# Attention steps on TensorE placed by shares of their stage's filling products

## The chip, the cores and the metric

The kernel runs on one core of one Trainium2 chip. The metric is the device time of one execution in microseconds (us); lower is better. The names of the engines are those of the profile: PE is TensorE, DVE is VectorE, ACT is ScalarE, POOL is GpSimd, SP issues the DMAs.

## The reference

One decoder block on 512 tokens of width 1024 in float32. A combined projection feeds two attention branches, multi-head latent attention (MLA, 8 heads) and differential attention (4 heads with two softmax maps each); their outputs are gated, merged and projected, and a SwiGLU layer of 2816 hidden channels follows.

```python
def apply_rope(x, positions, rot_dim):
...
def causal_attention(q, k, v):
...
def reference(...):
    xn = rmsnorm(x, norm_mix_g[l])
    proj = jnp.einsum('bsd,de->bse', xn, w_in[l])
    q_lat, kv_lat, k_rope, dq, dk, dv, gate_pre = jnp.split(proj, split_idx, axis=-1)
    q = jnp.einsum('bsr,re->bse', rmsnorm(q_lat, mla_q_norm_g[l]), mla_w_uq[l])
    kv = jnp.einsum('bsr,re->bse', rmsnorm(kv_lat, mla_kv_norm_g[l]), mla_w_ukv[l])
    ...
    o_mla = causal_attention(q_mla, k_mla, v_mla).reshape(B, S, MLA_WIDTH)
    ...
    o1 = causal_attention(dq[..., 0, :], dk[..., 0, :], dv)
    o2 = causal_attention(dq[..., 1, :], dk[..., 1, :], dv)
    ...
    o_diff = rmsnorm(o1 - lam * o2, diff_subln_g[l]) * (1.0 - lambda_init)
    gates = jax.nn.sigmoid(gate_pre + b_gate[l])
    merged = (g_mla * jnp.einsum('bse,ed->bsd', o_mla, w_branch_mla[l])
              + g_diff * jnp.einsum('bse,ed->bsd', o_diff, w_branch_diff[l]))
    x = x + jnp.einsum('bsd,de->bse', merged, w_out[l])
    hn = rmsnorm(x, norm_ffn_g[l])
    hid = jax.nn.silu(jnp.einsum('bsd,df->bsf', hn, w_ffn_gate[l])) * jnp.einsum('bsd,df->bsf', hn, w_ffn_up[l])
    x = x + jnp.einsum('bsf,fd->bsd', hid, w_ffn_down[l])
    return rmsnorm(x, norm_final_g)
```

## The kernel before

**Arithmetic.** Every large product is made of three matmuls in a rounded 32-bit format: the weights and the activations are each split into a high and a low part, and `mm3` (L299) issues high by high, high by low and low by high into one accumulation. A weight tile (512 KB or less) is loaded by SP into `raw`, its high part rounded by one engine (L264 or L266) and its low part formed by another (L269) into `w`. `w_eng` says which: DVE and POOL in the MLA stages, ACT and DVE in the differential stages.

**Stages.** After the start (input, latents, rotary tables) come four MLA stages, one for each pair of heads, and four differential stages, one for each head (loops at L807 and L819). Each stage traces its *filling products* first (`fill`, tables `FILL_MLA` and `FILL_DIFF`, L52 to L59): projections for later stages, 24 matmuls for each block of 128 columns of the input projection. Then it traces its *head steps* in an `urgent` block: `mla_head` twice, or `diff_norm` of the head before and `diff_head`. A head consists of four scores steps (`scores`, L624, one for each block of 128 queries, each followed by a reduction for the row maximum on DVE (L637), an exponential on ACT (L156) and a reciprocal (L640)), three groups of transposes (`transposed`, L651), each split on ACT and DVE, and the product with the values (`values` or the loop at L779). Behind the last stage the branch projections, the output projection and the SwiGLU layer follow, which are nearly all products.

**Order.** The program is written in tiles, and a scheduler puts each engine's instructions into one fixed order before the program runs. It takes what it holds ready by its own timeline, and among that what has the smaller priority number. `urgent` gives the head steps small numbers (from 1000), the rest counts from 1000000. So a head step goes ahead of any filling product as soon as the scheduler holds it ready. `tc.issue_after(x)` adds an edge: what is traced inside it stands behind `x` on `x`'s engine. The engines execute their orders strictly, and wait by semaphores.

**Buffers.** PSUM has three buffers for products (`ps_mm`), two for scores (`ps_sc`), two for transposes (`ps_tr`) and one for values (`ps_pv`). A step that needs a buffer waits until its last reader is done: a `ps_mm` of a differential query or key until the rotation (`rotate`, L562) has read it, which is a shuffle (L564) and a product (L565) on DVE; a `ps_sc` until the reduction at L637 has read it.

Of the kernel before, what the change touches and what calls it, by code (L numbers as in the profile page):

```python
# [93 lines left out]
def build(ctx, nc, tc, a, out):  # L94
# [176 lines left out]
    def weights(src, n0, n1, pick=None):  # L271
# [25 lines left out]
        return [w[:, i, :n].rearrange("p (a b) -> p a b", a=n0) for i in range(2)]  # L297

    def mm3(o, lhs, rhs, start, stop):  # L299
        (lh, ll), (rh, rl) = lhs, rhs  # L300
        nc.tensor.matmul(out=o, lhsT=lh, rhs=rh, start=start, stop=False)  # L301
        nc.tensor.matmul(out=o, lhsT=lh, rhs=rl, start=False, stop=False)  # L302
        return nc.tensor.matmul(out=o, lhsT=ll, rhs=rh, start=False, stop=stop)  # L303

# [318 lines left out]

    def scores(maps, i):  # L624


        n = (i + 1) * P
        pss = [PS("sc") for _ in maps]
        last = len(maps[0][0]) - 1
        for j in range(last + 1):  # L630
            for ps, (products, _) in zip(pss, maps):
                q, k = products[j]
                nc.tensor.matmul(out=ps[:, :n], lhsT=q[:, i * P:n], rhs=k[:, 0:n], start=j == 0, stop=j == last)  # L633
        rs = []
        for ps, (_, m) in zip(pss, maps):
            neg_max, s, r = sm(), sm(), sm()
            nc.vector.tensor_tensor_reduce(out=m, in0=ps[:, :n], in1=mask[:, S - n:], scale=-1.0, scalar=3.4e38,  # L637
                                           op0=ALU.add, op1=ALU.min, accum_out=neg_max)
            last_exp[0] = log_exp(out=m, in_=m, func=AF.Exp, bias=neg_max, scale=-1.0, accum_out=s)
            nc.vector.reciprocal(out=r, in_=s)  # L640
            rs.append(r)
        return rs
# [7 lines left out]

    def transposed(blocks):  # L651

        pt = T("PT", [P, 2, 1280], F32R)
        for js in ((0,), (1,), (2, 3)):
            ps = PS("tr")
            c = 0
            for j in js:
                for i in range(j, NB):
                    nc.tensor.transpose(out=ps[:, c:c + P], in_=blocks[i][:, j * P:(j + 1) * P], identity=ident)  # L659
                    c += P  # L660
            o0 = OFF[js[0]]
            split(ps[:, :c], pt[:, 0, o0:o0 + c], pt[:, 1, o0:o0 + c])
        return pt

    def values(pt, v):

        ps = PS("pv")
        for n_, (vs, s) in enumerate(((0, 0), (0, 1), (1, 0))):
            for j in range(NB):
                nc.tensor.matmul(out=ps[:, j * P:S], lhsT=v(j, vs), rhs=pt[:, s, OFF[j]:OFF[j] + S - j * P],  # L670
                                 start=n_ == 0 and j == 0, stop=n_ == 2 and j == NB - 1)
        return ps
# [6 lines left out]

    def diff_head(h, products):  # L680
        blocks = []
        for i, p1 in enumerate(prob_tiles()):
            p2 = T("P", [P, S], F32)[:, :(i + 1) * P]
            r1, r2 = scores(list(zip(products, (p1, p2))), i)
            nc.vector.tensor_mul(out=r2, in0=r2, in1=neg_lam)
            nc.scalar.activation(out=p2, in_=p2, func=AF.Copy, scale=r2)
            nc.vector.scalar_tensor_tensor(out=p1, in0=p1, scalar=r1, in1=p2, op0=ALU.mult, op1=ALU.add)
            blocks.append(p1)
        pt = transposed(blocks)
        ps = values(pt, lambda j, s: dv[(h // 2) * 2 + j // 2][:, s, (j % 2) * 256 + (h % 2) * P:  # L690
                                                              (j % 2) * 256 + (h % 2) * P + P])
        o32, sq = tmp(), tmp()
# [7 lines left out]

    def diff_norm(o32, sqs):

        ps = PS("tr")
        for s in range(2):
            nc.tensor.matmul(out=ps, lhsT=ones_r, rhs=sqs[s], start=s == 0, stop=s == 1)
        y, u = tmp(), tmp()
# [58 lines left out]

    def mla_head(qk, v, pair, o, h):
        q, k = qk[h]
        blocks = []
        for i, p in enumerate(prob_tiles()):
            r, = scores([([(q[0:96, a_, :], k[0:96, b_, :]) for a_, b_ in ((0, 0), (0, 1), (1, 0))], p)], i)  # L770
            if i in P_POOL:
# [3 lines left out]
            blocks.append(p)  # L775
        pt = transposed(blocks)
        c = 2 * (pair % 2) + h
        ps = PS("pv")
        for s in range(2):  # L779
            for j in range(NB):  # L780
                nc.tensor.matmul(out=ps[:, j * P:S], lhsT=v[j // 2][:, j % 2, c, :, :].rearrange("p s d -> p (s d)"),
                                 rhs=pt[:, s, OFF[j]:OFF[j] + S - j * P], start=s == 0 and j == 0,
                                 stop=s == 1 and j == NB - 1)
        u = tmp()[:64]
# [22 lines left out]
    for p in range(4):  # L807
        o = L_()
        o_mla.append(o)
        w_eng[:] = W_ENG  # L810
        fill(FILL_MLA[p])
        with urgent():
            for h in range(2):
                mla_head(mqk[p], mv[p // 2], p, o, h)
# [3 lines left out]
    w_eng[:] = W_ENG_DIFF  # L818
    for h in range(4):  # L819
        fill(FILL_DIFF[h])  # L820
        with urgent():
            if h > 0:
                o_diff.append(diff_norm(*parts[h - 1]))
            parts.append(diff_head(h, qk[h]))
    with urgent():
        o_diff.append(diff_norm(*parts[3]))

# [173 lines left out]
```

## Time and profile before

| | us |
|---|---|
| median of 3 runs | 751.91 (751.88 to 752.78) |
| the profiled execution, its own time | 753.9 |
| the profiled execution, span from first to last instruction | 752.1 |
| PE busy | 737.0 |
| DVE busy | 414.7 |
| ACT busy | 326.8 |
| MLA and differential stages, about | 75 to 310 |
| output projection and SwiGLU layer, about | 310 to 752 |

A row of the profile names a line of the kernel, an engine, an operation, the tile written and the tiles read. Busy time of PE counts each matmul until its result has drained, which overlaps with the start of the next; the pace of PE is read from the starts of successive matmuls. A 128x512 matmul has 0.39 us as its duration, and the next starts 0.23 us after it.

### The profile page before, as it was taken

To read this page: it belongs to the slowest core of one execution; us is meant where nothing else is said; L and a number is where in the kernel's file an instruction comes from. 1 tells how busy PE (TensorE), PEld (TensorE's weight loads), DVE (VectorE), ACT (ScalarE), POOL (GpSimd) and SP (SyncE) were. 2 spreads that over 40 slices of the span, in tenths; PEclk is the share of its full clock that TensorE was granted. 3 is DMA by queue.
4 is the path that set the end of the run, shared out by engine and by line. 5 is a ranking of instruction groups with operands and counts; after the bars stand their busy time and mean duration, and the time that the engine had idled before them with its cause. 6 is when DMAs were issued, how large, how long until landed. Compare 5 with 4: busy or idle time off the path is not lost.

```text
span 752.1 us, 9652 instructions
## 1 busy us (share of the span) xinstructions
PE 737.0 (98%) x3639; PEld 623.0 (83%) x3639; DVE 414.7 (55%) x800; ACT 326.8 (43%) x609; POOL 104.3 (14%) x94
## 2 busy tenths in 40 slices
PE   7999999999999999999999999999999999999996
PEld 5988889888888888788898888888888888888885
DVE  6968688898998745595453323333333332122424
ACT  6564558587667535644233323232322223122314
POOL 3505252631341001000000000000000000000302
PEclk9999999999999999999999999999999999999999
DMA  8404333552433322248023333333323232322203
GB/s 300 124 1 117 106 87 96 135 126 69 110 87 87 107 85 85 84 140 278 2 85 108 89 97 99 98 99 87 109 85 111 85 112 85 109 88 92 106 0 113
DMA packets 99820, 76.74 MB, mean 102 GB/s; under 512 B 6303, under 2 KB 86973, under 8 KB 99773
## 3 DMA queue, kind: packets, MB, share of 16 engines
q1 hardware_dynamic: 99773, 76.12, 34.3%
q8 instruction: 29, 0.48, 0.3%
q14 instruction: 18, 0.15, 0.1%
HBM read 69.81 MB, written 2.10 MB: 96 GB/s over the span
## 4 chain that ended last, share of the span: by engine, by line
PE 81%; DVE 9%; ACT 5%; POOL 2%; issue 2%; DMA 1%; SPq 0%; DVEq 0%; ACTq 0%
PE ps_mm L301 22%; PE ps_mm L303 22%; PE ps_mm L302 22%; PE ps_sc L633 2%; PE ps_sc L301 1%; PE ps_sc L302 1%; PE ps_tr L301 1%; PE ps_tr L302 1%; PE ps_tr L303 1%; PE ps_sc L303 1%; POOL t L567 1%; PE ps_tr L659 1%; ACT L L495 1%; DVE w L269 1%; DVE X L355 1%
## 5 line engine op out<-in xcount | busy, mean ns | idle before, releaser
L302 PE MATMUL ps_mm<-X,w 128*128 128x512 f32 (+1 forms) x568 | 217.0, 382 | 0.0
L301 PE MATMUL ps_mm<-X,w 128*128 128x512 f32 (+1 forms) x568 | 216.9, 382 | 0.1
L303 PE MATMUL ps_mm<-X,w 128*128 128x512 f32 (+1 forms) x568 | 216.6, 382 | 0.0
L269 DVE TENSOR_TENSOR w<-raw,w 128x1024 fp32r<-128x1024 f32 x92 | 116.3, 1266 | 165.4 <-ACT w L264 165.2
L264 ACT ACTIVATE w<-raw 128x1024 fp32r<-128x1024 f32 (+1 forms) x98 | 101.1, 1036 | 181.2 <-issue 78.9
L303 PEld LDWEIGHTS ps_mm<-X,w 128*128 128x128 f32 x568 | 106.9, 188 | 19.9 <-POOL w L269 0.3
L301 PEld LDWEIGHTS ps_mm<-X,w 128*128 128x128 f32 x568 | 106.7, 188 | 19.9 <-DVE t L565 0.2
L302 PEld LDWEIGHTS ps_mm<-X,w 128*128 128x128 f32 x568 | 106.8, 188 | 19.7 <-DVE X L255 0.2
L936 POOL TENSOR_TENSOR L<-L,P 128x512 f32<-128x512 f32 (+1 forms) x9 | 11.6, 1299 | 439.0 <-ACT t L935 439.0
L909 ACT ACTIVATE t<-ps_mm 128x512 f32<-128x512 f32 x22 | 13.2, 598 | 80.9 <-PE ps_mm L303 80.9
L910 DVE TENSOR_TENSOR t<-t,ps_mm 128x512 f32<-128x512 f32 x22 | 15.1, 688 | 59.7 <-PE ps_mm L303 59.7
L156 ACT ACTIVATE P<-P,sm 128x128 f32<-128x128 f32 (+3 forms) x64 | 35.8, 560 | 27.4 <-DVE sm L637 27.0
L269 POOL TENSOR_TENSOR w<-raw,w 128x1024 fp32r<-128x1024 f32 (+3 forms) x22 | 37.3, 1701 | 57.5 <-PE ps_tr L472 25.8
L633 PE MATMUL ps_sc<-L,L 96*128 96x128 f32 (+7 forms) x160 | 36.5, 327 | 1.5 <-DVE sm L637 1.5
L302 PE MATMUL ps_mm<-w,L 128*128 128x512 f32 (+1 forms) x100 | 37.2, 372 | 0.0
L301 PE MATMUL ps_mm<-w,L 128*128 128x512 f32 (+1 forms) x100 | 37.2, 374 | 0.0
L303 PE MATMUL ps_mm<-w,L 128*128 128x512 f32 (+1 forms) x100 | 37.1, 373 | 0.0
L301 PE MATMUL ps_mm<-L,w 128*128 128x512 f32 x90 | 35.2, 393 | 0.5 <-ACT w L264 0.5
L302 PE MATMUL ps_mm<-L,w 128*128 128x512 f32 x90 | 35.5, 394 | 0.0
L303 PE MATMUL ps_mm<-L,w 128*128 128x512 f32 x90 | 35.2, 393 | 0.0
L251 ACT ACTIVATE L<-t 64x512 fp32r<-64x512 f32 (+2 forms) x47 | 29.1, 623 | 13.6 <-POOL t L567 6.2
L255 DVE TENSOR_TENSOR L<-t,L 128x512 fp32r<-128x512 f32 (+2 forms) x37 | 29.6, 801 | 4.8 <-ACT L L251 4.5
(265 smaller groups left out, 1231.9 us busy)
## 6 DMA issues: line engine op xcount, KB each, us to landing
raw<-w_in SPq DMA_DIRECT2D x28, 512.0 KB, 4.0
raw<-w_ffn_gate SPq DMA_DIRECT2D x22, 512.0 KB, 3.9
raw<-w_ffn_up SPq DMA_DIRECT2D x22, 512.0 KB, 3.9
raw<-w_ffn_down SPq DMA_DIRECT2D x22, 512.0 KB, 3.6
L<-L SPq DMA_DIRECT2D x32, 128.0 KB, 2.9
raw<-w_out SPq DMA_DIRECT2D x8, 512.0 KB, 3.7
L<-x SPq DMA_DIRECT2D x8, 256.0 KB, 6.1
raw<-w_branch_mla SPq DMA_DIRECT2D x4, 512.0 KB, 3.4
```

The source lines that it names most:

```text
L156: return nc.scalar.activation(**kw)
L251: nc.scalar.activation(out=hi, in_=src, func=AF.Copy, scale=scale)
L255: nc.vector.tensor_sub(out=lo, in0=src, in1=r32(hi))
L264: nc.scalar.activation(out=o, in_=i, func=AF.Copy)
L269: (nc.vector if w_eng[1] == 'dve' else nc.gpsimd).tensor_sub(out=o, in0=i, in1=r32(hi))
L301: nc.tensor.matmul(out=o, lhsT=lh, rhs=rh, start=start, stop=False)
L302: nc.tensor.matmul(out=o, lhsT=lh, rhs=rl, start=False, stop=False)
L303: return nc.tensor.matmul(out=o, lhsT=ll, rhs=rh, start=False, stop=stop)
L633: nc.tensor.matmul(out=ps[:, :n], lhsT=q[:, i * P:n], rhs=k[:, 0:n], start=j == 0, stop=j == last)
L909: last_silu = nc.scalar.activation(out=g, in_=gate_ps, func=AF.Silu)
L910: nc.vector.tensor_mul(out=g, in0=g, in1=ps)
L936: nc.gpsimd.tensor_mul(out=xs, in0=xs, in1=g)
```

## The change

Each stage now keeps a list of its filling products (`units`, the last matmul of each `mm3`; emptied at the start of a stage). Each head step on PE is traced inside `paced(at)`, which is an `issue_after` edge to the product that stands at the share `at` of that list. For an MLA pair the shares are 0 to 0.54 for the first head and 0.28 to 0.97 for the second, so that the second head's steps stand between those of the first. For differential heads the four scores steps have 0, 0.14, 0.28 and 0.42, the transposes 0.7, 0.7 and 0.8, the values 0.95 (all times 0.6 for the last head), and the norm of the head before 0.2, 0.2 and 0.12; the norm of the last head has 0.75. A share of 0 adds no edge. Nothing that is computed changes.

```diff
@@ -296,11 +296,19 @@
             n = n0 * nk
         return [w[:, i, :n].rearrange("p (a b) -> p a b", a=n0) for i in range(2)]
 
+    units = []
+
     def mm3(o, lhs, rhs, start, stop):
         (lh, ll), (rh, rl) = lhs, rhs
         nc.tensor.matmul(out=o, lhsT=lh, rhs=rh, start=start, stop=False)
         nc.tensor.matmul(out=o, lhsT=lh, rhs=rl, start=False, stop=False)
-        return nc.tensor.matmul(out=o, lhsT=ll, rhs=rh, start=False, stop=stop)
+        units.append(nc.tensor.matmul(out=o, lhsT=ll, rhs=rh, start=False, stop=stop))
+        return units[-1]
+
+    def paced(at):
+
+        n = int(at * len(units))
+        return tc.issue_after(units[n - 1].ins) if n > 0 else nullcontext()
 
     def norm_transpose(xt, g, dst, t, junk):
 
@@ -621,7 +629,7 @@
         return kpe
 
 
-    def scores(maps, i):
+    def scores(maps, i, at):
 
 
         n = (i + 1) * P
@@ -630,7 +638,8 @@
         for j in range(last + 1):
             for ps, (products, _) in zip(pss, maps):
                 q, k = products[j]
-                nc.tensor.matmul(out=ps[:, :n], lhsT=q[:, i * P:n], rhs=k[:, 0:n], start=j == 0, stop=j == last)
+                with paced(at):
+                    nc.tensor.matmul(out=ps[:, :n], lhsT=q[:, i * P:n], rhs=k[:, 0:n], start=j == 0, stop=j == last)
         rs = []
         for ps, (_, m) in zip(pss, maps):
             neg_max, s, r = sm(), sm(), sm()
@@ -648,27 +657,29 @@
         for i in (2, 3):
             yield T("P", [P, S], F32)[:, :(i + 1) * P]
 
-    def transposed(blocks):
+    def transposed(blocks, at):
 
         pt = T("PT", [P, 2, 1280], F32R)
-        for js in ((0,), (1,), (2, 3)):
+        for at_, js in zip(at, ((0,), (1,), (2, 3))):
             ps = PS("tr")
             c = 0
             for j in js:
                 for i in range(j, NB):
-                    nc.tensor.transpose(out=ps[:, c:c + P], in_=blocks[i][:, j * P:(j + 1) * P], identity=ident)
+                    with paced(at_):
+                        nc.tensor.transpose(out=ps[:, c:c + P], in_=blocks[i][:, j * P:(j + 1) * P], identity=ident)
                     c += P
             o0 = OFF[js[0]]
             split(ps[:, :c], pt[:, 0, o0:o0 + c], pt[:, 1, o0:o0 + c])
         return pt
 
-    def values(pt, v):
+    def values(pt, v, at):
 
         ps = PS("pv")
         for n_, (vs, s) in enumerate(((0, 0), (0, 1), (1, 0))):
             for j in range(NB):
-                nc.tensor.matmul(out=ps[:, j * P:S], lhsT=v(j, vs), rhs=pt[:, s, OFF[j]:OFF[j] + S - j * P],
-                                 start=n_ == 0 and j == 0, stop=n_ == 2 and j == NB - 1)
+                with paced(at):
+                    nc.tensor.matmul(out=ps[:, j * P:S], lhsT=v(j, vs), rhs=pt[:, s, OFF[j]:OFF[j] + S - j * P],
+                                     start=n_ == 0 and j == 0, stop=n_ == 2 and j == NB - 1)
         return ps
 
 
@@ -677,18 +688,18 @@
     eps = sb.tile([P, 1], F32, name="eps")
     nc.gpsimd.memset(eps, EPS)
 
-    def diff_head(h, products):
+    def diff_head(h, products, span):
         blocks = []
         for i, p1 in enumerate(prob_tiles()):
             p2 = T("P", [P, S], F32)[:, :(i + 1) * P]
-            r1, r2 = scores(list(zip(products, (p1, p2))), i)
+            r1, r2 = scores(list(zip(products, (p1, p2))), i, span * (0, 0.14, 0.28, 0.42)[i])
             nc.vector.tensor_mul(out=r2, in0=r2, in1=neg_lam)
             nc.scalar.activation(out=p2, in_=p2, func=AF.Copy, scale=r2)
             nc.vector.scalar_tensor_tensor(out=p1, in0=p1, scalar=r1, in1=p2, op0=ALU.mult, op1=ALU.add)
             blocks.append(p1)
-        pt = transposed(blocks)
+        pt = transposed(blocks, (span * 0.7, span * 0.7, span * 0.8))
         ps = values(pt, lambda j, s: dv[(h // 2) * 2 + j // 2][:, s, (j % 2) * 256 + (h % 2) * P:
-                                                              (j % 2) * 256 + (h % 2) * P + P])
+                                                              (j % 2) * 256 + (h % 2) * P + P], span * 0.95)
         o32, sq = tmp(), tmp()
         nc.scalar.activation(out=o32, in_=ps, func=AF.Copy)
         nc.scalar.activation(out=sq, in_=ps, func=AF.Square)
@@ -698,11 +709,12 @@
         nc.gpsimd.tensor_sub(out=sqs[1], in0=sq, in1=r32(sqs[0]))
         return o32, sqs
 
-    def diff_norm(o32, sqs):
+    def diff_norm(o32, sqs, at):
 
         ps = PS("tr")
         for s in range(2):
-            nc.tensor.matmul(out=ps, lhsT=ones_r, rhs=sqs[s], start=s == 0, stop=s == 1)
+            with paced(at):
+                nc.tensor.matmul(out=ps, lhsT=ones_r, rhs=sqs[s], start=s == 0, stop=s == 1)
         y, u = tmp(), tmp()
         log_exp(out=y, in_=ps, func=AF.Ln, scale=1.0 / P, bias=eps)
         last_exp[0] = log_exp(out=y, in_=y, func=AF.Exp, scale=-0.5)
@@ -764,23 +776,27 @@
         return v
 
     def mla_head(qk, v, pair, o, h):
+
+        at = ((0, 0.07, 0.14, 0.21, 0.36, 0.36, 0.43, 0.54), (0.28, 0.46, 0.58, 0.65, 0.8, 0.8, 0.86, 0.97))[h]
         q, k = qk[h]
         blocks = []
         for i, p in enumerate(prob_tiles()):
-            r, = scores([([(q[0:96, a_, :], k[0:96, b_, :]) for a_, b_ in ((0, 0), (0, 1), (1, 0))], p)], i)
+            r, = scores([([(q[0:96, a_, :], k[0:96, b_, :]) for a_, b_ in ((0, 0), (0, 1), (1, 0))], p)], i,
+                         at[i])
             if i in P_POOL:
                 nc.gpsimd.tensor_scalar(out=p, in0=p, scalar1=r, scalar2=0.0, op0=ALU.mult, op1=ALU.add)
             else:
                 nc.scalar.activation(out=p, in_=p, func=AF.Copy, scale=r)
             blocks.append(p)
-        pt = transposed(blocks)
+        pt = transposed(blocks, at[4:7])
         c = 2 * (pair % 2) + h
         ps = PS("pv")
         for s in range(2):
             for j in range(NB):
-                nc.tensor.matmul(out=ps[:, j * P:S], lhsT=v[j // 2][:, j % 2, c, :, :].rearrange("p s d -> p (s d)"),
-                                 rhs=pt[:, s, OFF[j]:OFF[j] + S - j * P], start=s == 0 and j == 0,
-                                 stop=s == 1 and j == NB - 1)
+                with paced(at[7]):
+                    nc.tensor.matmul(out=ps[:, j * P:S], lhsT=v[j // 2][:, j % 2, c, :, :].rearrange("p s d -> p (s d)"),
+                                     rhs=pt[:, s, OFF[j]:OFF[j] + S - j * P], start=s == 0 and j == 0,
+                                     stop=s == 1 and j == NB - 1)
         u = tmp()[:64]
         nc.scalar.activation(out=u, in_=ps[64:P, :], func=AF.Copy)
         nc.vector.tensor_add(out=u, in0=ps[0:64, :], in1=u)
@@ -808,6 +824,7 @@
         o = L_()
         o_mla.append(o)
         w_eng[:] = W_ENG
+        units.clear()
         fill(FILL_MLA[p])
         with urgent():
             for h in range(2):
@@ -817,13 +834,14 @@
     o_diff, parts = [], []
     w_eng[:] = W_ENG_DIFF
     for h in range(4):
+        units.clear()
         fill(FILL_DIFF[h])
         with urgent():
             if h > 0:
-                o_diff.append(diff_norm(*parts[h - 1]))
-            parts.append(diff_head(h, qk[h]))
+                o_diff.append(diff_norm(*parts[h - 1], (0, 0.2, 0.2, 0.12)[h]))
+            parts.append(diff_head(h, qk[h], (1, 1, 1, 0.6)[h]))
     with urgent():
-        o_diff.append(diff_norm(*parts[3]))
+        o_diff.append(diff_norm(*parts[3], 0.75))
 
 
     sigmoids(last_exp[0], (0, 1))
```

What the edges do to the order is shown at one place, the border between the last MLA stage and the first differential stages, on PE and on DVE. The names there: `ps_mm_412` and `ps_mm_420` are the query and key products of differential head 2 and `ps_mm_425` is a gate product (all three are the fill of the stage of differential head 0); `ps_mm_476` is the first product of the next stage's fill. `ps_pv_408` is the value product of the last MLA head, `ps_sc_438` to `ps_sc_459` are the scores of differential head 0, `ps_tr_467` and `ps_tr_468` its transposes, and `ps_sc_500` is the first scores step of differential head 1. Lines are those of each kernel: L633 before is L642 after, L637 is L646, L564 and L565 are L572 and L573, L781 is L797.

PE before, from the values of the last MLA head on:

```order
L781 MATMUL ps_pv_408_2106<-PT_404_2086,L_221_1412 128x256
L781 MATMUL ps_pv_408_2106<-PT_404_2086,L_221_1412 128x128
L659 MATMUL ps_tr_467_2331<-ident_98,P_446_2284 128x128
L659 MATMUL ps_tr_468_2338<-ident_98,P_427_2239 128x128
L659 MATMUL ps_tr_468_2338<-ident_98,P_446_2284 128x128
L633 MATMUL ps_sc_500_2536<-L_354_1909,L_352_1907 128x128
L633 MATMUL ps_sc_500_2536<-L_354_1909,L_353_1908 128x128
L302 MATMUL ps_mm_425_2212<-X_2_63,w_424_2209 128x512
L303 MATMUL ps_mm_425_2212<-X_2_63,w_424_2209 128x512
L301 MATMUL ps_mm_425_2212<-X_2_63,w_424_2209 128x512
L302 MATMUL ps_mm_425_2212<-X_2_63,w_424_2209 128x512
L303 MATMUL ps_mm_425_2212<-X_2_63,w_424_2209 128x512
```

PE after, from the same step on:

```order
L797 MATMUL ps_pv_408_2106<-PT_404_2086,L_221_1412 128x128
L797 MATMUL ps_pv_408_2106<-PT_404_2086,L_219_1396 128x512
L797 MATMUL ps_pv_408_2106<-PT_404_2086,L_219_1396 128x384
L669 MATMUL ps_tr_467_2331<-ident_98,P_427_2239 128x128
L797 MATMUL ps_pv_408_2106<-PT_404_2086,L_221_1412 128x256
L797 MATMUL ps_pv_408_2106<-PT_404_2086,L_221_1412 128x128
L669 MATMUL ps_tr_468_2338<-ident_98,P_427_2239 128x128
L642 MATMUL ps_sc_459_2310<-L_290_1659,L_288_1657 128x512
L642 MATMUL ps_sc_459_2310<-L_290_1659,L_289_1658 128x512
L642 MATMUL ps_sc_500_2536<-L_354_1909,L_352_1907 128x128
L642 MATMUL ps_sc_500_2536<-L_354_1909,L_353_1908 128x128
L303 MATMUL ps_mm_476_2375<-X_1_62,w_475_2372 128x512
```

Before, the first step of head 1 (`ps_sc_500`) is followed by matmuls of `ps_mm_425`. After, all of `ps_mm_425` stands ahead of the first of these rows, the last scores of head 0 (`ps_sc_459`) have moved down to here, and `ps_mm_476` follows `ps_sc_500` at once.

DVE before, from the reduction of `ps_sc_458` on (two names at a time are output and input; a row of an ISA instruction with one name is the read-out of a row maximum):

```order
L637 ISA P_456_2307,sm_460_2315<-ps_sc_458_2309,mask_103 128x512
L637 ISA sm_460_2315 128x1
L269 TENSOR_TENSOR w_483_2419<-raw_482_2417,w_483_2419 128x1024
L640 RECIPROCAL sm_462_2317<-sm_461_2316 128x1
L637 ISA P_457_2308,sm_463_2321<-ps_sc_459_2310,mask_103 128x512
L637 ISA sm_463_2321 128x1
L640 RECIPROCAL sm_465_2323<-sm_464_2322 128x1
L564 STREAM_SHUFFLE t_414_2151<-ps_mm_412_2125 128x512
L685 TENSOR_TENSOR sm_465_2323<-sm_465_2323,neg_lam_286 128x1
L565 TENSOR_TENSOR t_413_2150<-ps_mm_412_2125,tab0_548 128x512
L564 STREAM_SHUFFLE t_422_2198<-ps_mm_420_2172 128x512
L565 TENSOR_TENSOR t_421_2197<-ps_mm_420_2172,tab0_548 128x512
```

DVE after, from the reduction of `ps_sc_449` on:

```order
L646 ISA P_447_2285,sm_453_2298<-ps_sc_449_2287,mask_103 128x384
L646 ISA sm_453_2298 128x1
L269 TENSOR_TENSOR w_488_2459<-raw_487_2457,w_488_2459 128x1024
L649 RECIPROCAL sm_455_2300<-sm_454_2299 128x1
L646 ISA P_456_2307,sm_460_2315<-ps_sc_458_2309,mask_103 128x512
L646 ISA sm_460_2315 128x1
L572 STREAM_SHUFFLE t_414_2151<-ps_mm_412_2125 128x512
L573 TENSOR_TENSOR t_413_2150<-ps_mm_412_2125,tab0_548 128x512
L572 STREAM_SHUFFLE t_422_2198<-ps_mm_420_2172 128x512
L573 TENSOR_TENSOR t_421_2197<-ps_mm_420_2172,tab0_548 128x512
L802 TENSOR_TENSOR t_409_2115<-ps_pv_408_2106,t_409_2115 64x512
L696 TENSOR_TENSOR sm_455_2300<-sm_455_2300,neg_lam_286 128x1
```

The rotation of `ps_mm_412` (shuffle and product) follows the reductions of both scores of the last query block before; after, it stands between the reduction of `ps_sc_458` and that of `ps_sc_459`, and the forming of a weight's low part (L269) stands ahead of the reduction of `ps_sc_458`.

More of the change, by code (lines that the diff above doesn't have):

```diff
@@ L1 @@
 import math
-from contextlib import ExitStack
+from contextlib import ExitStack, nullcontext
 import numpy as np
```

## The prediction

> **What bounds the kernel now.** I read the head of the page first, then a table by stretch of the span, then the list of what TensorE (PE) waited for, then single places.
>
> ```profile
> PE 737.0 (98%) x3639; PEld 623.0 (83%) x3639; DVE 414.7 (55%) x800; ACT 326.8 (43%) x609; POOL 104.3 (14%) x94
> ```
>
> PE is busy for 737.0 of 752.1 us, so at most 15.1 us can be won anywhere by order alone. The table by stretch says where they lie. Its columns are the stretch, its length, then busy time and instructions of PE, weight loads, VectorE (DVE), ScalarE (ACT) and GpSimd (POOL), then the granted clock.
>
> ```profile
> 0.00:20.00 20.00, 15.83 (x78) 12.08 (x79) 13.69 (x43) 13.16 (x35) 7.16 (x17) 0.91 0.90 301
> 76.24:79.66 3.42, 1.93 (x14) 1.43 (x12) 3.36 (x6) 1.68 (x4) 3.09 (x2) 1.00 0.74 184
> 79.66:83.07 3.41, 3.41 (x16) 3.41 (x17) 2.34 (x9) 1.80 (x5) 0.85 (x2) 0.50 0.91 263
> 98.00:112.00 14.00, 13.71 (x90) 12.37 (x88) 13.02 (x25) 7.32 (x17) 7.29 (x5) 1.00 0.29 78
> 112.00:183.00 71.00, 71.00 (x414) 62.63 (x415) 61.27 (x151) 51.75 (x117) 27.59 (x24) 1.00 0.46 112
> 183.00:200.00 17.00, 17.00 (x86) 14.26 (x85) 15.67 (x36) 11.33 (x23) 6.54 (x4) 1.00 0.41 102
> 200.00:263.00 63.00, 62.95 (x310) 52.78 (x309) 54.62 (x135) 41.95 (x88) 13.18 (x9) 1.00 0.35 92
> 740.00:752.10 12.10, 5.27 (x24) 4.03 (x22) 6.85 (x21) 5.66 (x17) 4.27 (x4) 0.86 0.47 174
> ```
>
> The first 20 us and the last 12 hold 4.2 + 6.8 = 11.0 of the 15.1 us, and the change touches neither. The program order of PE is the same in both kernels up to its 530th matmul, a scores step of the second MLA pair that stands near 98 us, and again from the last steps of differential head 3 on, near 285 us. Between 98 and 263 us PE idles 0.29 + 0.05 us. That is the first finding: **there is almost nothing left for this change to win.** The second is the DVE column: 61.27 of 71.00, 15.67 of 17.00, 54.62 of 63.00. DVE is nearly as full as PE there. PE does not wait for it only because there is always a product to put between two attention steps. An order that uses those products up at the wrong place will wait for DVE.
>
> ```profile
> PE ps_sc L633 <- DVE sm L637: 1.5, 1, 1.5
> PE ps_mm L303 <- DVE X L355: 1.1, 1, 1.1
> PE ps_pv L781 <- DVE PT L255: 0.3, 1, 0.3
> ```
>
> The 1.5 us wait (at 77 us, in the first MLA stage) lies ahead of the first changed row. It stays, with what follows it: PE idles 3.42 - 1.93 = 1.49 us in the stretch 76.24 to 79.66, and in the next 3.41 us the granted clock is 0.50. The price of that drop is read from the starts of equal matmuls.
>
> ```profile
> 76.46 0.28 PE L302 MATMUL ps_mm<-w,X 128*128 128x256 f32 x1
> 76.58 0.28 PE L303 MATMUL ps_mm<-w,X 128*128 128x256 f32 x1
> ...
> 80.58 0.41 PE L302 MATMUL ps_mm<-w,X 128*128 128x256 f32 x1
> 80.79 0.41 PE L303 MATMUL ps_mm<-w,X 128*128 128x256 f32 x1
> ```
>
> They start 0.12 us apart at full clock and 0.21 in the drop: 16 of them take 3.41 us and would take 1.92, so **one drop costs 1.5 us.**
>
> **The change part by part.** No instruction is added on a compute engine: as many matmuls, vector and scalar operations as before. The added edges are between instructions of PE itself, so they cost no semaphore; only the order moves.
>
> *What it removes.* The one wait of PE that the changed stretch holds, 0.3 us at 111.9 (the row above; a few tenths more are lost in slots around it). I take -0.4 us, with 0 and -0.6 as ends. SP's and GpSimd's queues hold the same entries. On SP three loads of weights move ahead by one or two places, past two copies of rotary key rows, two of query rows and one load of the final gain; on GpSimd scalings and weight roundings of the MLA pairs change places. An issue there takes SP some 0.4 to 0.6 us and the DMA share is at most 0.46 in these stretches, so I cost that at nothing; it is covered as long as the buffer that the load fills is free, and costs the copies behind it that wait if not.
>
> *What it moves, and what that uncovers.* The pacing holds the second MLA head of a pair back to as much as 0.97 of its stage, so the tail of the last MLA head comes about one product (24 matmuls) later, into the fill of differential head 0. There three queues meet: that tail, head 0's own score steps (due at 0 to 0.42 of the fill, now overdue), and head 1's first step, which has share 0 and is not held at all. The rows of order in the change's section show it: before, `ps_mm_425` still has 11 matmuls to go behind `ps_sc_500`. After, all of `ps_mm_425` has been issued, and from `ps_sc_449` to `ps_mm_476` PE has only attention steps. Both ends of this run wait for DVE: `ps_sc_500` for a score buffer (two of them), which the reduction of `ps_sc_458` frees; `ps_mm_476` for a product buffer (three), which the rotation's shuffle and product on `ps_mm_412` free. What DVE must do in between, in the order after, has these rows in the trace of before:
>
> ```profile
> 181.62 0.54 DVE L637 CUSTOM_DVE_ANT_0 P<-ps_sc,mask 128x384 f32<-128x384 f32 x1
> 182.09 0.08 DVE L637 DVE_READ_ACCUMULATOR2_ANT sm<- 128x1 f32 x1
> ...
> 185.19 1.22 DVE L269 TENSOR_TENSOR w<-raw,w 128x1024 fp32r<-128x1024 f32 x1
> 186.33 0.15 DVE L640 RECIPROCAL sm<-sm 128x1 f32<-128x1 f32 x1
> 186.40 0.67 DVE L637 CUSTOM_DVE_ANT_0 P<-ps_sc,mask 128x512 f32<-128x512 f32 x1
> 187.00 0.08 DVE L637 DVE_READ_ACCUMULATOR2_ANT sm<- 128x1 f32 x1
> ...
> 188.05 0.73 DVE L564 STREAM_SHUFFLE t<-ps_mm 128x512 f32<-128x512 f32 x1
> 188.68 0.14 DVE L685 TENSOR_TENSOR sm<-sm,neg_lam 128x1 f32<-128x1 f32 x1
> 188.74 0.68 DVE L565 TENSOR_TENSOR t<-ps_mm,tab 128x512 f32<-128x512 f32 x1
> ```
>
> From start to start: reduction of `ps_sc_449` 0.47, rounding of a weight tile 1.14, reciprocal 0.07, reduction of `ps_sc_458` 0.60 and its read-out 0.08: 2.36 us from the end of `ps_sc_449` until `ps_sc_500` may go. Then shuffle 0.63 and product 0.68: 1.31 us more until `ps_mm_476` may go. What PE has meanwhile is priced by these rows:
>
> ```profile
> 184.21 0.62 PE L633 MATMUL ps_sc<-L,L 128*128 128x512 f32 x2
> 184.66 0.39 PE L301 MATMUL ps_mm<-X,w 128*128 128x512 f32 x1
> ...
> 185.71 0.99 PE L781 MATMUL ps_pv<-PT,L 128*128 128x256 f32 x6
> 186.54 0.51 PE L659 MATMUL ps_tr<-ident,P 128*128 128x128 f32 x3
> 186.80 0.42 PE L633 MATMUL ps_sc<-L,L 128*128 128x128 f32 x2
> ```
>
> Two pairs of 512-wide scores 0.45 each, six value products 0.83, two transposes 0.17: 1.90 us, of which about 0.15 run before `ps_sc_449` has ended. So PE is out of work after 1.75 us and idles 2.36 - 1.75 = 0.6, with a hand-over of about 0.06 us each way 0.7. Then it issues the two small scores (about 0.12 us before the next may start) and idles again, 1.31 + 0.06 - 0.12 = 1.25. **Sum 2.0 us.** The ends: if DVE has done the rounding (1.14) before `ps_sc_449` ends, only about 1.25 stays or, with the rotation earlier too, nothing; if DVE comes late to `ps_sc_449`, its lateness is added. Before, it came 2.0 us late (PE row at 179.11 below, DVE row at 181.62), which nobody noticed. So the ends are 0 and 4.0, and I take 2.0, since the chain of rows above is the nearest to the new order and DVE has less in its queue ahead of that step.
>
> ```profile
> 179.11 0.51 PE L633 MATMUL ps_sc<-L,L 128*128 128x384 f32 x2
> 179.46 0.57 PE L781 MATMUL ps_pv<-PT,L 128*128 128x512 f32 x2
> ```
>
> *What the wait does to the clock.* Two idle stretches of 0.7 and 1.25 us with 0.1 us between them are 2.0 us of idle in 2.1. In this trace 1.49 us of idle in 3.42 was followed by 3.41 us at 0.50, while the next row, with 3.41 - 2.33 = 1.08 us idle in as long a stretch, was not.
>
> ```profile
> 28.46:31.87 3.41, 2.33 (x14) 2.01 (x13) 3.41 (x10) 0.75 (x4) 2.31 (x3) 1.00 0.52 133
> ```
>
> Whether the new idle time falls into one such stretch or is cut in two by its border is chance; as 2.1 us fit whole into 3.41 in one case of three and a part over about 1.3 us remains in most others, I take a second drop as likelier than not: +1.5 us, with 0 as the other end. The Trainium skill speaks against this term: TensorE: Matmul & The Clock Gate, in "Why this matters for your kernels", asks only that idle gaps above some 3 us between bursts be avoided. The trace does not agree, since 1.49 us sufficed at 77 us; by the page's rule the sum would lack the 1.5 us, which is the second rival.
>
> **Sum.** 751.9 - 0.4 + 2.0 + 1.5 = 755.0 us. The same terms on the profiled execution's span, 752.1, give 755.2; its own time was 753.9, 2.0 above the median of the three runs, and I put the terms on the median, since a difference is what they are.
>
> **The rivals.** (1) *Forecast: the wait, and a drop of the clock behind it*: 755.0. Chance 0.48. (2) *The wait without a drop*, because the idle time is split or too short: 751.9 - 0.4 + 2.0 = 753.5. For it speaks that 1.08 us left the clock alone; against it that the new gap is nearly twice that. Chance 0.24. (3) *No new wait, so not slower*: DVE gets to the rounding and the rotation before PE has used up `ps_mm_425`. It decides at one point: DVE must be 2.0 us further along when `ps_sc_449` ends than the order puts it. Then only the 0.4 us remain: 751.5. For it speaks that DVE was free enough before; against it that the shuffle stands behind the reduction of `ps_sc_458`, whose scores PE itself issues only in this run. Chance 0.16. (4) *DVE is late as before*, 2.0 us, so that the wait is 4.0 and the drop certain: 751.9 - 0.4 + 4.0 + 1.5 = 757.0. Chance 0.09. (5) *Faster*: the new timing after 98 us cannot undo the wait at 77 us, and 0.6 us is all that the changed stretch holds; over 0.2% (1.5 us) would need a drop of the clock that this profile shows to be missing in the runs. Chance 0.03.
>
> **How the numbers follow.** About 0.2%, 1.5 us, is what a measurement of this kernel can tell from no change: slower means above 753.4, faster below 750.4. Slower: 0.48 + 0.09 and two thirds of rival 2 (753.5 lies at the border) give 0.73; faster 0.03; the same 0.24. The range goes from rival 3 (751.5, less 0.1) to a wait of a little under 4 us (756.8): it leaves out half of rival 4 and the faster cases, and the edges of rival 3, under 0.2 together.
>
> **What would show each step.** Right: PE's list of waits after has `ps_sc` (its line is 642) for the reduction and a product for the rotation (lines 572 and 573), some 0.7 and 1.2 us near 183 to 190 us; the row of 0.3 us for `ps_pv` is gone; the table by stretch has a 3.41 us stretch at 0.50 right behind that wait besides the one at 79.66. The wait of 1.5 us at 77 us is as before. Wrong: PE busy without a gap from 98 to 285 us (rival 3), the gap with the clock at 1.00 behind it (rival 2), or new waits at other attention steps, which nothing in these rows foresees.

## The result, and the profile after

| | us, median of the runs | lowest to highest |
|---|---|---|
| before (6 runs beside it) | 751.89 | 751.69 to 752.83 |
| changed (6 runs) | 755.70 | 755.53 to 756.91 |

The ratio is 1.0051, with a 95% interval of 1.0041 to 1.0062: the change makes the kernel 3.8 us slower. The profiled execution of the changed kernel took 756.69 us, its span is 754.9.

The head of the page and the table by stretch, in the columns of the prediction (stretch, length, busy time of PE, weight loads, DVE, ScalarE, GpSimd, then granted clock):

```profile
PE 738.7 (98%) x3639; PEld 623.9 (83%) x3639; DVE 413.2 (55%) x800; ACT 326.3 (43%) x609; POOL 102.2 (14%) x94
```

```profile
98.00:112.00 14.00, 13.43 (x94) 12.30 (x93) 13.82 (x24) 7.21 (x16) 7.24 (x4) 1.00 0.43 106
112.00:183.00 71.00, 71.00 (x408) 62.21 (x408) 59.97 (x144) 50.73 (x112) 26.95 (x24) 1.00 0.43 106
183.00:200.00 17.00, 15.47 (x71) 12.51 (x70) 15.04 (x39) 11.65 (x24) 5.46 (x4) 0.90 0.38 94
200.00:263.00 63.00, 63.00 (x312) 53.01 (x311) 52.21 (x134) 40.08 (x88) 11.37 (x8) 1.00 0.33 87
188.33:191.74 3.41, 1.88 (x9) 1.25 (x8) 3.41 (x11) 1.17 (x3) 1.61 (x2) 1.00 0.55 140
191.74:195.16 3.42, 3.42 (x10) 2.64 (x9) 3.29 (x8) 2.70 (x6) 3.42 (x3) 0.50 0.08 21
```

One stretch carries the loss. From 183 to 200 us PE idles 17.00 - 15.47 = 1.53 us, where it idled nothing before, and its mean clock there is 0.90: the last two rows show 1.53 us idle and then 3.42 us at 0.50. A smaller new loss stands in 98 to 112 us, 0.57 us idle against 0.29. PE's list of waits names them:

```profile
PE ps_sc L642 <- DVE sm L646: 2.2, 2, 1.5
PE ps_mm L303 <- DVE t L573: 0.8, 1, 0.8
PE ps_mm L304 <- POOL w L269: 0.6, 1, 0.6
```

The first row holds the old wait of 1.5 us at 77 us and a second of 0.74; the other two are new. The 0.3 us row for `ps_pv` is gone. PE's timeline at the border of the last MLA head, differential head 0 and head 1, and then what DVE does meanwhile (start, time, operation; in brackets the idle time before it and what ended it):

```profile
187.93 0.72 PE L642 MATMUL ps_sc<-L,L 128*128 128x512 f32 x2
189.38 0.44 PE L642 MATMUL ps_sc<-L,L 128*128 128x128 f32 x2 [0.74 <-DVE sm L646]
190.61 0.50 PE L303 MATMUL ps_mm<-X,w 128*128 128x512 f32 x1 [0.79 <-DVE t L573]
...
192.40 0.63 PE L303 MATMUL ps_mm<-X,w 128*128 128x512 f32 x1
192.83 0.63 PE L304 MATMUL ps_mm<-X,w 128*128 128x512 f32 x1
```

```profile
186.69 0.56 DVE L646 CUSTOM_DVE_ANT_0 P<-ps_sc,mask 128x384 f32<-128x384 f32 x1 [0.57 <-PE ps_sc L642]
...
187.43 1.23 DVE L269 TENSOR_TENSOR w<-raw,w 128x1024 fp32r<-128x1024 f32 x1 [0.18 <-ACT w L264]
188.58 0.15 DVE L649 RECIPROCAL sm<-sm 128x1 f32<-128x1 f32 x1
188.65 0.67 DVE L646 CUSTOM_DVE_ANT_0 P<-ps_sc,mask 128x512 f32<-128x512 f32 x1
...
189.25 0.73 DVE L572 STREAM_SHUFFLE t<-ps_mm 128x512 f32<-128x512 f32 x1
189.88 0.67 DVE L573 TENSOR_TENSOR t<-ps_mm,tab 128x512 f32<-128x512 f32 x1
```

By starts, the two 512-wide scores need 0.45 and the next step follows after 1.45, so 1.00 us is lost; the two small scores need 0.12 and the product follows after 1.23, so 1.11 is lost. Together 2.1 us. In the drop the products start 0.43 us apart.

### The profile page after: what moved, and what is told of

It reads as the page before. It is cut to its first block, busy times and chain, and to the rows that moved or that the text cites. A ratio compares the mean times of both kernels' runs of the same rounds, so it can differ in the third digit from the quotient of the medians.

```text
span 754.9 us, 9638 instructions
## 1 busy us (share of the span) xinstructions
PE 738.7 (98%) x3639; PEld 623.9 (83%) x3639; DVE 413.2 (55%) x800; ACT 326.3 (43%) x609; POOL 102.2 (14%) x94
## 4 chain that ended last, share of the span: by engine, by line
PE 89%; DVE 4%; ACT 3%; DMA 1%; issue 1%; POOL 1%; SPq 1%; DVEq 0%; POOLq 0%
PE ps_mm L303 24%; PE ps_mm L304 24%; PE ps_mm L305 24%; PE ps_sc L642 3%; PE ps_tr L669 2%; DMA w<-w_in 1%; PE ps_sc L305 1%; PE ps_sc L303 1%; PE ps_tr L305 1%; PE ps_tr L303 1%; PE ps_tr L304 1%; PE ps_sc L304 1%; ACT L L503 1%; PE ps_pv L797 1%; PE ps_pv L681 1%
## 5 line engine op out<-in xcount | busy, mean ns | idle before, releaser
L269 DVE TENSOR_TENSOR w<-raw,w 128x1024 fp32r<-128x1024 f32 x92 | 115.5, 1258 | 164.9 <-ACT w L264 164.5
L269 POOL TENSOR_TENSOR w<-raw,w 128x1024 fp32r<-128x1024 f32 (+3 forms) x22 | 37.3, 1702 | 55.1 <-PE ps_tr L480 25.8
L642 PE MATMUL ps_sc<-L,L 96*128 96x128 f32 (+7 forms) x160 | 36.8, 326 | 2.2 <-DVE sm L646 2.2
L646 DVE CUSTOM_DVE_ANT_0 P<-ps_sc,mask 128x128 f32<-128x128 f32 (+3 forms) x64 | 30.6, 478 | 7.2 <-PE ps_sc L642 7.0
```

Source lines behind the costliest of these rows:

```text
L269: (nc.vector if w_eng[1] == 'dve' else nc.gpsimd).tensor_sub(out=o, in0=i, in1=r32(hi))
```

## The experiments

All ratios are to runs of the kernel before on the same chip, with 95% intervals.

**Which of the two pacings makes the loss.** Two kernels, each with one part of the change undone.

```diff
-        at = ((0, 0.07, 0.14, 0.21, 0.36, 0.36, 0.43, 0.54), (0.28, 0.46, 0.58, 0.65, 0.8, 0.8, 0.86, 0.97))[h]
+        at = (0,) * 8
```

> The MLA heads are not held at all (all their shares 0), the differential heads are held as in the change. Theory: the shares of the MLA heads push the tail of the last MLA head into the fill of differential head 0, and all of the loss comes from that border. Then there is no gap of PE between 183 and 200 us, no extra wait for GpSimd at 105 us, the 0.3 us wait on ps_pv near 111 us is back, and the time is that of before: 751.9 (751.4 to 752.6), 3.8 us below the change. Rival 1, the held steps of the differential heads make the wait: 755.7, with the gaps of 0.7 and 0.8 us near 190 still there. Rival 2, the loss is spread over many places: between, 753 to 754.5.

Measured: 752.40 us (11 runs), ratio 1.0002 (0.9993 to 1.0011). The 0.3 us wait on `ps_pv` is back, and PE has no gap at the border:

```profile
183.00:200.00 17.00, 17.00 (x86) 14.36 (x85) 16.15 (x38) 11.37 (x24) 5.55 (x4) 1.00 0.37 94
```

The other one frees the differential heads:

```diff
-                o_diff.append(diff_norm(*parts[h - 1], (0, 0.2, 0.2, 0.12)[h]))
-            parts.append(diff_head(h, qk[h], (1, 1, 1, 0.6)[h]))
+                o_diff.append(diff_norm(*parts[h - 1], 0))
+            parts.append(diff_head(h, qk[h], 0))
...
-        o_diff.append(diff_norm(*parts[3], 0.75))
+        o_diff.append(diff_norm(*parts[3], 0))
```

> The differential heads are not held at all (all their shares 0), the MLA heads are held as in the change. Theory (MLA shares make the loss): the two gaps at 189 to 191 us stay, 0.7 behind the reduction and 0.8 behind the rotation, 1.5 to 2.0 us in all, and the time is that of the change, 755.7 (755.0 to 757.0). Rival 1 (the differential heads' shares): no gap there, 751.9.

Measured: 755.24 us (5 runs), ratio 1.0050 (1.0037 to 1.0062), with the rows for `ps_sc` (2.2 us in 2) and for the rotation (0.8) as in the change. The whole loss belongs to the shares of the MLA heads; those of the differential heads neither cost nor gain anything that these runs can tell.

**Which pair.** Four kernels with shares for some pairs only. The first frees the last pair:

```diff
+        at = (0,) * 8 if pair == 3 else at
```

> As the change, but the two heads of the last MLA pair have share 0. Theory A (the prediction's wording): the share of 0.97 of the last pair's second head holds its tail back; without it the tail runs earlier, no gap at 187 to 191 us, and the time falls to 752 to 752.5. Theory B: the steps of the last pair come late anyway, since the pairs before it were held and each step queues behind those; its own shares hold nothing. Then the order and the two gaps (0.9 and 1.0 us in slots of PE) stay, and the time is that of the change, 754.4 to 756.

Measured: 755.51 us (4 runs), ratio 1.0044 (1.0030 to 1.0057). Theory B holds: by the two traces four scores steps of the last pair move ahead by three to five matmuls (20 rows between 146 and 164 us), from there on PE's order is row for row that of the change, and the waits are the same. The others pace one pair alone, `at = at if pair in (1,) else (0,) * 8` and so on:

> As the change, but of the four MLA pairs only pair 1 (the second) is held; the differential heads are held as in the change. Theory: lateness made in one stage is carried to the border only if the stages behind it cannot take it up; pair 1 makes the 0.6 us wait for GpSimd at 104 us, and the free pairs 2 and 3 catch up, so there is no gap at 187 to 191 us: 751.8 + 0.7 - 0.3 = 752.2 (751.8 to 752.8). Rival: any held pair makes the tail late, gap of 1.9 us, 754.4 to 755.7.

> As the change, but of the MLA pairs only pair 2 (the third) is held. Theory: its late steps push those of pair 3 behind their fill, and the last tail meets the differential heads' steps: gaps of 1.9 us or more in all between 183 and 192 us, 754.4 to 756.5. Rival (pair 3's own shares are needed, or pairs 1 and 2 together): no gap, 752.

> As the change, but of the MLA pairs only pair 3 (the last) is held. Theory: its own shares are enough to bring the tail one product later too, though they are not needed: idle of 1.9 to 2.4 us near 189 us, 754.4 to 755.7. Rival: without the lateness of the pairs before, the tail is in time and there is no gap, 752.

| paced pair | us, runs | ratio | idle of PE at the border |
|---|---|---|---|
| 1 alone | 751.83, 10 | 0.9992 (0.9983 to 1.0002) | none |
| 2 alone | 757.48, 4 | 1.0060 (1.0045 to 1.0075) | 0.6 + 0.8, and 0.4 for ScalarE |
| 3 alone | 755.57, 8 | 1.0036 (1.0024 to 1.0048) | one gap, row below |

The runs of before beside these three had 752.75 as their median, as more of them held a drop of the clock (8 of 17 at a clock of 0.996 or less; see below). Pair 2 alone came out 1 us above its range; its gaps sum to 1.8 us, close to the 1.9 expected, and the rest was not traced.

```profile
PE ps_mm L303 <- DVE t L573: 2.2, 1, 2.2
```

That is the wait of PE with pair 3 alone: one of 2.2 us for the rotation. So pair 2's or pair 3's shares are each enough, pair 1's are not: two free stages follow it, and PE has no gap at the border. Beside the pairs ahead of it, the shares of pair 3 add nothing to the loss, since its steps are late already. Pair 0 was not run alone with the shares of the change; with larger ones (below) the border has no gap.

**What VectorE is late with.** The prediction blamed the sum of its own rows, the 1.14 us of rounding above all. The first kernel gives the roundings of low halves in the fill of differential head 0 to GpSimd:

```diff
+        w_eng[:] = W_ENG_DIFF if h else ['act', 'pool']
         fill(FILL_DIFF[h])
```

> As the change, but the low halves of the weights in the fill of differential head 0 are made by GpSimd and not by VectorE. Theory (a chain of VectorE rows of 2.36 and then 1.3 us at the border, 1.14 to 1.23 of it the rounding): the wait of ps_sc for the reduction (0.74 to 0.9 us) goes, the wait of the product for the rotation (0.8 to 1.2) stays. PE then idles 0.8 to 1.2 us there, less than the 1.49 that was followed by half the clock, so the drop behind it goes too: 755.7 - 0.8 - 1.5 = 753.4 (752.8 to 754.0); if the drop stays, 754.9. Rival (the reduction is late because of its own scores or ScalarE, not because of the rounding ahead of it): both gaps stay, 755.7 or, with GpSimd slowing VectorE, more.

Measured: 756.48 us (5 runs), ratio 1.0057 (1.0044 to 1.0071): a miss, with both gaps still there, as the rival had it. The wait of `ps_sc` did not go but grew to 1.20 us. DVE's timeline there shows why:

```profile
189.33 0.68 DVE L646 CUSTOM_DVE_ANT_0 P<-ps_sc,mask 128x512 f32<-128x512 f32 x1
189.94 0.08 DVE L646 DVE_READ_ACCUMULATOR2_ANT sm<- 128x1 f32 x1
190.91 0.16 DVE L649 RECIPROCAL sm<-sm 128x1 f32<-128x1 f32 x1 [0.88 <-ACT P L156]
190.99 0.67 DVE L646 CUSTOM_DVE_ANT_0 P<-ps_sc,mask 128x512 f32<-128x512 f32 x1
```

Between the two reductions no rounding stands, and yet they start 1.66 us apart: the reciprocal of the first softmax stands ahead of the second reduction in DVE's queue and waits 0.88 us for ScalarE's exponential. In the changed kernel the rounding fills that wait and lasts 0.6 us longer, since ScalarE is done at 187.81 + 0.19 = 188.00 and the reciprocal starts at 188.58:

```profile
187.31 0.60 ACT L156 ACTIVATE P<-P,sm 128x384 f32<-128x384 f32 x1
187.81 0.19 ACT L156 ACTIVATION_READ_ACCUMULATOR P<-P,sm 128x1 f32 x1
```

The order of the scores moved too in the kernel with GpSimd's roundings (two 512-wide steps stand ahead of the gap, not one), so it is no clean removal. The second kernel leaves the reciprocals out, with the row sums in their place, in the last MLA pair and in differential heads 0 and 1:

```diff
-            nc.vector.reciprocal(out=r, in_=s)
-            rs.append(r)
+            skip[0] or nc.vector.reciprocal(out=r, in_=s)
+            rs.append(s if skip[0] else r)
```

> As the change, but the last MLA pair and differential heads 0 and 1 leave the reciprocal of the row sums out (the sums themselves stand in its place), some 24 instructions of VectorE of 0.07 us each. Theory A: at the border VectorE's next reduction queues behind a reciprocal that waits for ScalarE's exponential (0.7 to 0.9 us after each reduction), and that serial chain, not the sum of VectorE's own work, makes the gap. Then the gaps at 187 to 191 us shrink from 1.9 to about 0.7 us, no half clock follows there, and the time is 753.3 (752.6 to 754.5). Theory B: the gap is the sum of VectorE's rounding, reductions and rotation; a reciprocal is 0.07 us, so the gap stays at 1.7 to 1.9 us and the time at 755.3.

Measured: 752.32 us (10 runs), ratio 1.0006 (0.9997 to 1.0015), 1.0 us under the expected value of theory A and 0.3 under its range. The MLA shares are all in place, and the wait for the reduction is gone; of the rotation's, 0.24 us is left:

```profile
187.29 0.69 DVE L646 CUSTOM_DVE_ANT_0 P<-ps_sc,mask 128x512 f32<-128x512 f32 x1 [0.73 <-PE ps_sc L642]
187.91 0.08 DVE L646 DVE_READ_ACCUMULATOR2_ANT sm<- 128x1 f32 x1
188.15 0.29 DVE L646 CUSTOM_DVE_ANT_0 P<-ps_sc,mask 128x128 f32<-128x128 f32 x1 [0.16 <-PE ps_sc L642]
```

Now DVE waits for PE, with 0.86 us from one reduction to the next. Twenty-four instructions of 0.07 us cannot do that by their own time. But this kernel does not single out the reciprocal: without it the planner also put other steps at other places. PE has products between the two scores steps (three from 187.09 on), and no rounding stands between the two reductions any more (the nearest start at 182.91 and 190.85). How much of the loss is the reciprocal's wait, and how much the order, is not shown.

**What half the clock needs.** The changed kernel was run again for a second trace:

> The changed kernel again, for a second trace and the granted clocks. Theory: PE idles over 1.5 us inside or across one 3.41 us stretch at 189 to 191 us in every execution, so the 3.41 us at half clock behind it come in nearly all, and the time is 755.5 to 756.9. Rival: where the border of the stretches falls differs from execution to execution, the drop comes in some only, and the runs fall in two groups, 1.1 to 1.5 us apart, with a mean clock of 0.995 and 0.991 to 0.993.

Measured: 755.42 us (5 runs), ratio 1.0045 (1.0032 to 1.0057). The rival holds in kind, with three groups where it named two, at other clocks. Every run's mean granted clock is known; the 11 runs of the changed kernel and the 15 of before beside this one fall into groups:

| | clock | us |
|---|---|---|
| before, 10 runs | 0.997 to 0.999 | 751.55 to 751.94 |
| before, 5 runs | 0.993 to 0.996 | 752.73 to 753.64 |
| changed, 2 runs | 0.999 | 754.42, 754.44 |
| changed, 7 runs | 0.995 to 0.997 | 755.42 to 756.11 |
| changed, 2 runs | 0.991 | 756.69, 756.91 |

In the new trace, one of the two at 0.999, the same gaps stand and no drop follows:

```profile
187.70:191.11 3.41, 1.97 (x9) 1.59 (x10) 3.41 (x10) 0.82 (x2) 2.01 (x2) 1.00 0.62 154
191.11:194.53 3.42, 3.42 (x17) 2.84 (x16) 3.28 (x7) 3.10 (x6) 3.42 (x3) 1.00 0.03 7
```

All drops of a trace stand on one grid of 3.41 us, at another place in each execution, and a drop fills the stretch behind the one that idled. Here the grid cut 0.1 us of idle off. To see more of the dose, one kernel held the first MLA pair alone, by larger shares:

```diff
+        at = (0,)*8 if pair else ((0.1,.2,.3,.4,.5,.5,.6,.7),(.3,.4,.5,.6,.8,.8,.86,.97))[h]
```

> As the change, but only the first MLA pair is held, by larger shares (0.1 to 0.7 and 0.3 to 0.97); the other pairs have share 0. It lengthens the wait near 77 us to about 2.0 us, to see what idle time brings half the clock. Theory: at about 1.5 us of idle in one stretch of 3.41 us the drop comes in some executions only (before: few of 15), at 2.0 us in nearly all. Then the granted clock of most runs is 0.996 or less (before: 0.998 in most), and the time is 751.9 + 0.5 + 1.3 = 753.7 (753.0 to 754.2). Rival: drops come at random, whatever the length; most runs at 0.998 and a time of 752.4.

Measured: 756.97 us (5 runs), ratio 1.0063 (1.0048 to 1.0078), clock 0.993 to 0.995 in all five. So every run has a drop, as the theory on the clock had it; the time was missed by 3 us, as a second gap that I had not foreseen, 2.5 us near 114 us, brought a drop of its own in the profiled run:

```profile
76.64:80.05 3.41, 1.45 (x12) 1.48 (x13) 3.09 (x9) 1.34 (x4) 2.03 (x3) 1.00 0.87 235
80.05:83.46 3.41, 3.41 (x17) 3.41 (x17) 0.73 (x3) 0.23 (x2) 0.48 (x1) 0.50 0.71 191
114.19:117.60 3.41, 1.33 (x11) 1.36 (x12) 2.77 (x9) 3.34 (x8) 0.00 (x0) 1.00 0.11 22
117.60:121.01 3.41, 3.41 (x17) 3.31 (x16) 2.00 (x7) 2.07 (x7) 0.43 (x2) 0.50 0.00 0
```

The two runs at 0.995 took 756.04 and 756.38 us, the three others 756.97 or more. At 0.0023 a drop (see the next section) this points to one drop fewer there, so that one of the two gaps brought none, though both hold about 2 us in the trace. Where the grid cuts a gap may decide, as in the changed kernel; those two runs have no trace, so it is not shown.

**The wait at 77 us**, which neither kernel touches, was looked into for its own sake. In the trace of before DVE, GpSimd and PE stand there like this:

```profile
75.90 2.43 POOL L269 TENSOR_TENSOR w<-raw,w 128x1024 fp32r<-128x1024 f32 x1 [0.63 <-DVE w L266]
...
76.34 2.20 DVE L266 CAST w<-raw 128x384 fp32r<-128x384 f32 x1
...
78.47 0.27 DVE L637 CUSTOM_DVE_ANT_0 P<-ps_sc,mask 128x128 f32<-128x128 f32 x1
...
78.80 0.79 PE L633 MATMUL ps_sc<-L,L 96*128 96x384 f32 x3 [1.47 <-DVE sm L637]
```

```profile
L266 DVE CAST w<-raw 128x384 fp32r<-128x384 f32 x4 | 3.2, 810 | 0.3 <-PE ps_mm L303 0.3
```

The second fence is the group of that rounding (busy time, mean ns, idle time before): four take 3.2 us, so the other three take 0.35 on average, and this one, which ends 0.2 us after GpSimd's (78.54 and 78.33), 2.20. One edit of the kernel before gives that stage's high halves to ScalarE:

```diff
-        w_eng[:] = W_ENG
+        w_eng[:] = W_ENG if p else ['act', 'pool']
```

> The kernel before (no pacing) with one edit: in the stage of the first MLA pair the high halves of the weights are rounded by ScalarE and not by VectorE. Theory: the 1.5 us wait near 77 us comes from a rounding of 128x384 on VectorE that takes 2.20 us beside GpSimd's rounding of the low halves (0.3 to 0.4 us without it); with it gone PE does not wait there, and no half clock can follow it in any run: 751.9 - 1.4 = 750.5 (750.0 to 751.0), below both kernels. Rival: ScalarE is late in turn, or GpSimd's own tile is, and the wait only changes its name: 751.5 to 752.5.

Measured: 749.85 us (7 runs), ratio 0.9972 (0.9961 to 0.9983), 2.0 us below the kernel before, 5.9 below the changed one and 0.15 below the expected range. The row for `ps_sc` is not in PE's list of waits any more, and PE has no gap from 72 to 82 us, where it idled 10.00 - 8.51 = 1.49 us before (first the kernel before, then this one):

```profile
72.00:82.00 10.00, 8.51 (x47) 7.50 (x46) 9.21 (x16) 3.67 (x9) 6.68 (x6) 0.88 0.81 209
72.00:82.00 10.00, 10.00 (x71) 9.16 (x70) 5.52 (x17) 7.42 (x17) 6.56 (x5) 1.00 0.86 225
```

The wait is 1.5 of the 2.0 us. PE's order moved here too (57 rows between 76 and 103 us), so the remaining 0.5 us may come from that; it was not traced.

## Why the prediction was right, and where not

755.0 was forecast and 755.7 measured, within the range of 751.4 to 756.8 and on the likeliest side, slower. That the sum is so close is partly luck: one term was 0.7 us too low, and another 0.2 to 0.4 too high.

- **Little to win** (PE busy 737.0 of 752.1): borne out. The wait at 77 us stayed. The first changed row was named too late: in the traces the orders part at PE's 517th matmul, at 95 us, and not near 98; PE idles nowhere between, so no term changes.
- **What it removes**, -0.4 us: mis-sized, in sign too. The `ps_pv` wait went, but the same stretch got another, 0.6 us for a weight tile from GpSimd at 105 us. GpSimd's rounding and the product that waits for it:

```profile
103.81 2.39 POOL L269 TENSOR_TENSOR w<-raw,w 128x1024 fp32r<-128x1024 f32 x1 [1.83 <-DVE w L266]
...
106.25 0.39 PE L304 MATMUL ps_mm<-w,X 128*128 128x256 f32 x1 [0.57 <-POOL w L269]
```

  Idle time from 98 to 112 us rose from 0.29 to 0.57, so this term is +0.3. The prediction had said that GpSimd's roundings change places and put that at nothing; the 0.6 us show that they are not covered. With pair 1 alone the same row stands in PE's list, so it comes from that pair's shares.
- **The wait at the border**, +2.0 us: right in place, rows and size, 2.1 us by the starts (0.74 and 0.79 in the brackets, where 0.7 and 1.2 were named).
- **What holds DVE**: the chain was read from the order correctly, but its cause was put too simply. It is not the sum of DVE's rows alone: with the rounding out of it, the reciprocal waited for ScalarE instead (0.88 us).
- **Whose share**: "The pacing holds the second MLA head of a pair back to as much as 0.97 of its stage, so the tail of the last MLA head comes about one product later" is right for pair 3 alone. In the change it names the wrong holder: freed, the last pair's tail comes no sooner, and the order at the border is the same.
- **The clock**, +1.5 us: right in kind, a little too large. By the groups, a changed kernel without a drop inside the span takes 754.43 and the median run 755.6, so the term is about 1.1 in the median, 0 in 2 of 11 runs. "It stays, with what follows it", of the drop behind the wait at 77 us, was wrong for most runs: a drop of 3.41 us at half clock takes 0.0023 off a run's mean clock, and 10 of the 15 runs of before (0.997 to 0.999) have no room for one beside the one at the very end that each trace shows. So its median holds none, and its profiled execution, at 0.993, is of the other kind (it has drops at 11 and at 80 us). That took nothing from the sum, since the terms were put on the median.

So +3.8 splits into about 2.5 of waits (754.43 - 751.9; 2.1 and 0.3 of it are found in the rows above) and 1.1 to 1.3 of clock; forecast were 1.6 and 1.5. The traces give the same split: from PE's 450th to its 1600th matmul, about 87 to 301 us, the kernel before takes 213.9 us, the changed kernel 216.4 in the trace without a drop and 217.6 in the one with a drop there. Idle time of 1.5 us in one stretch was enough again: in the traces of the changed kernel, of the one with free differential heads and of the one with a free last pair, 1.53 us stand ahead of a drop at the border. The Trainium skill (TensorE: Matmul & The Clock Gate, "Why this matters for your kernels") warns only of gaps above some 3 us; by that rule the last row of the table by stretch would have the clock 1.00, and it has 0.50.

## What to carry to other kernels

Holding steps back to a share of the fill can pay only where the stage has idle time to lose; in a full one it can move steps across the stage's border, where they meet the next stage's, and a hold in one stage can be paid one or two stages later. Read the in-order queues at that border for an instruction that waits for another engine: what stands behind it waits too, however short it is. Compare traces only with the granted clock of the run beside them, since a drop that comes in a third of the runs looks like a part of the kernel.

## What the runs showed of the hardware

- **Idle time and the granted clock.** Over all traces, and between the first and the last instruction: behind stretches of 3.41 us with 1.95 to 2.24 us idle a drop followed each time (seven stretches); with 1.42 to 1.69 us one did in some and not in others, at one place too (1.49 at 77 us: a drop in the trace of before, none in the second trace of the changed kernel); with 1.40 or less, none. What decides in between, the runs don't tell.
- **VectorE beside GpSimd.** A rounding of 0.35 us took 2.20 while GpSimd's ran, and at 105 us in the changed kernel one that reads and writes SBUF alone took this long:

```profile
104.47 2.29 DVE L257 SCALAR_TENSOR_TENSOR L<-t,L 128x512 fp32r<-128x512 f32 x1
```

  In the trace of before both of this kind together take 1.4 us. The Trainium skill (SBUF — State Buffer, "SBUF: two separate sides") calls the pair of ports that the two engines share an exclusive lock, held for the whole instruction; these rows agree within 0.15 us: GpSimd's end and then the operation's own time come to 78.33 + 0.35 = 78.68 where the first ended at 78.54, and to 106.20 + 0.68 = 106.88 where the second ended at 106.76.
